# Mixture-of-experts units in another order: the units of two experts behind the three fixed ones, the five largest experts last

## The chip, the cores and the metric

One core of a Trainium2 chip runs the kernel. The metric is the device time of one execution in microseconds (us); lower is better. The kernel before takes 544.43 us, the median of three runs (543.29 to 544.66).

## The reference

One layer of a hybrid decoder trunk for 512 tokens of width 1024: a token-mixing part (convolution, RG-LRU and gated linear attention side by side), and then a mixture of 16 experts in 4 groups. Each token picks one group and two experts in it. Only the second part is touched by the change:

```python
def hier_moe(h, w_rg, b_rg, w_re, b_re, w_gate, w_up, w_down):
    ...
    y = jnp.zeros_like(h)
    for g in range(N_GROUPS):
        a = jnp.einsum("bsd,edf->bsef", h, w_gate[g])
        up = jnp.einsum("bsd,edf->bsef", h, w_up[g])
        hid = jax.nn.silu(a) * up * comb[:, :, g, :, None]
        y = y + jnp.einsum("bsef,efd->bsd", hid, w_down[g])
    return y
```

An expert has gate and up weights of 1024 x 512 and down weights of 512 x 1024, all in float32. The trunk's output is x plus both parts, with a last RMS norm.

## The kernel before

The first half of the time is the token mixing and the routing; the expert part runs from about 264 us to the end. On the chip the kernel counts how many tokens each expert has, sorts the thirteen experts that are not fixed by that count, and treats the experts as twelve **units**, one after the other (the loop over `u`, from about L1500):

- units 0 to 2 are the experts 0 to 2 (`NS` = 3, fixed, so that their weights can be loaded before the routing is known);
- units 3 to 7 are the five largest of the others (`NB` = 5), one expert each;
- units 8 to 11 are the eight smallest in pairs, 64 token slots for each of the two.

`alone(u)` tells a unit of one expert from a pair; `cols_of(u)` gives the ranks of a unit's experts, and the weights are named by rank: `raw_g40` is the first half of the gate weights of rank 4 (ranks 0 to 2 are the fixed experts), `raw_u` and `raw_d` are up and down.

**Weights.** An expert's weights are six chunks of 1 MB (two each of gate, up and down). All 96 chunks are loaded on SP's queue by `load_chunk` (L964) in the order in which the units use them, into a ring of 17 buffers (`nring`); a chunk's load is issued when the chunk 17 places before it has been used, and at most three loads (`AHEAD`) are in flight together.

**A unit of one expert** computes in split float32: every quarter of its weights is cast to a high part on ACT (`mh_...`, L87), and DVE takes the rest into a low part (`ml_...`, L88); the tokens are split likewise (`xh`, `xl`). Each product is three matmuls, high weights x high tokens (L82), low x high (L83) and high x low (L84). Of the down weights the last quarter stays plain float32 (L1449), save in the units that `full(u)` names. **A pair** uses the plain float32 weights as they were loaded: two experts' tokens stand side by side, 64 rows each, and each matmul works on one half of the columns of the PE array (`rows_of(a)`), gate and up at L1412, down at L1458. DVE splits nothing for a pair. In the trace a float32 matmul is two instructions.

**Order inside the loop.** In step `u`: gate projection of unit `u` into `pga`; the hidden values of unit `u-1` are turned (`pht`, L1420); up projection of unit `u` into `pup`; token slots and one-hots of unit `u+3` (`ptb`, `pwt`); the tokens of unit `u+1` are turned (`pgt`, L1381); the down projection of unit `u-1` (`pd`) and, from its result, `ye` on DVE (`scaled`, L1486) which is scattered to the tokens by GpSimd; then `sact` of unit `u`. The program is written in this order, but a scheduler sets the order of the instructions on each engine; an engine then works its own list strictly in that order.

**The end.** The last two units are not scattered: their results are put back into token order by matmuls with a one-hot matrix (`pf`, L1584), added to the rows read back from memory (`back_add`), normalised and stored. The down projection of the last unit is interleaved by hand with these.

Of the kernel before, what the change touches and what calls it, by code (L numbers as in the profile page):

```python
# [20 lines left out]
NT = T // P  # L21
# [3 lines left out]
KE = DE // P  # L25
# [12 lines left out]
NS = 3  # L38
NB = 5
ND = NE - NS  # L40
HALF = P // 2
HELD = 15
EARLY = 12


@with_exitstack
def trunk_kernel(
# [7 lines left out]
    nc = tc.nc  # L55
# [190 lines left out]
    for i in range(NT):  # L246
# [11 lines left out]
        for hf in range(2):  # L258
            pt = big(f"pxt{i}{hf}")
            for kk in range(4):  # L260
                k = hf * 4 + kk
# [110 lines left out]
    for kd in range(KD):  # L372
# [10 lines left out]
        if kd in (1, 2, 4):  # L383
            n = kd // 2 + 1
# [216 lines left out]
    both = range(2)  # L601
# [325 lines left out]

    NU = NS + NB + (ND - NB) // 2

    def alone(u):  # L930
        return u < NS + NB

    def cols_of(u):
        c = u if alone(u) else 2 * u - NS - NB
        return (c,) if alone(u) else (c, c + 1)

# [7 lines left out]
    raws = {}  # L946
# [183 lines left out]
    for i in range(NT):  # L1130
        for j in range(i + 1):
            nc.tensor.matmul(pp[:, i * NE:(i + 1) * NE], utri if j == i else onesb, chob[:, j, :],
                             start=(j == 0), stop=(j == i))
# [105 lines left out]
        nc.vector.tensor_reduce(swt[:, u:u + 1], pwt[:, 0:3], axis=AX.X, op=ALU.add)  # L1239

    def halves_of(u):
        n = 2 * (u - NS - NB)
        return shalf[:, n:n + 1], shalf[:, n + 1:n + 2]

    def unit_slots(u, oh):
# [43 lines left out]
    with tc.If(many > 0):  # L1289
        bcast(gt2, mod_dram[3])  # L1290
        with tc.tile_pool(name="ov", bufs=1) as ov:
# [6 lines left out]
            with tc.For_i(0, NE, 1) as e:  # L1298
# [12 lines left out]
                with tc.For_i(0, NT, 1):  # L1311
# [11 lines left out]
                    for hf in range(2):  # L1323
                        pt = small(f"ov_pt{hf}")
                        for kk in range(4):
                            k = hf * 4 + kk
# [34 lines left out]
    with ExitStack() as ms:  # L1361
        me = ms.enter_context(tc.tile_pool(name="me", bufs=2, reuse_waits="tile"))
        used = [0]
# [52 lines left out]
        def hid_t(u, hid):  # L1416
            pt = small(f"pht{u}")
            hv = hid.rearrange("s (p k) -> s p k", k=KE)
            for k in range(KE):
                nc.tensor.transpose(pt[:, k * P:(k + 1) * P], hv[:, :, k], ident)  # L1420
            pt = pt.rearrange("p (k t) -> p k t", k=KE)
            if not alone(u):
                ht = me.tile([P, KE, P], F32, tag="hh", bufs=2, name=f"ht{u}")
                nc.scalar.copy(ht, pt)  # L1424
                return None, None, ht
            n = KE if full(u) else KE - 1
            hh = me.tile([P, KE, P], F32R, tag="hh", bufs=2, name=f"hh{u}")[:, 0:n, :]
            hlo = me.tile([P, KE, P], F32R, tag="hlo", bufs=1, name=f"hlo{u}")[:, 0:n, :]
            nc.scalar.copy(hh, pt[:, 0:n, :])
            nc.vector.tensor_tensor(hlo, pt[:, 0:n, :], hh.bitcast(F32), ALU.subtract)  # L1430
            if full(u):
                return hh, hlo, None
            ht = me.tile([P, P], F32, tag="ht", bufs=1, name=f"ht{u}")
            nc.scalar.copy(ht, pt[:, KE - 1, :])
            return hh, hlo, ht

        def down(u, hs):

            ps = [big(f"pd{u}{i}") for i in range(2)]
            hh, hlo, ht = hs  # L1440

            def cols(hf):
                return slice(hf * 512, hf * 512 + 512)

            if alone(u):
                for k, (hi, lo) in enumerate(quarters()):
                    for hf in range(2):
                        if lo is None:
                            nc.tensor.matmul(ps[hf], ht, hi[:, 0, cols(hf)], start=False, stop=True)  # L1449
                        else:  # L1450
                            mm3(ps[hf], hh[:, k, :], hlo[:, k, :], hi[:, 0, cols(hf)], lo[:, 0, cols(hf)],
                                k == 0, k == KE - 1)
                    yield ps
                return

            def both(k, hf):
                for a in range(2):
                    nc.tensor.matmul(ps[hf][rows_of(a)], ht[:, k, rows_of(a)],  # L1458
                                     raws[used[0] + k // 2 * 2 + a][:, k % 2, cols(hf)],
                                     start=(k == 0), stop=(k == KE - 1))  # L1460
            if u == NU - 1:
                for hf in range(2):
                    for k in range(KE):
                        both(k, hf)
                        yield ps[hf]
                return
            for k in range(KE):
                for hf in range(2):
                    both(k, hf)
                yield ps  # L1470
            spent(4)
# [119 lines left out]
        def half15(hf, ps):  # L1591
            cols = slice(hf * 512, hf * 512 + 512)
            nc.vector.tensor_tensor(y15[:, cols], ps, gt2[:, cols], ALU.mult)
            part(p15, y15, hf)

        def back_add(i, hf):
            back(i, hf, oh15, p15, False)
            cols = slice(hf * 512, hf * 512 + 512)
            xi = xo[i][:, 0, cols]
            nc.vector.tensor_tensor(xi, xi, pf[i, hf], ALU.add)  # L1600
            nc.scalar.activation(xo[i][:, 1, cols], xi, AF.Square, scale=D ** -0.5, accum_out=sq[:, i, hf:hf + 1])
# [10 lines left out]
                nc.sync.dma_start(out[i * P:(i + 1) * P, cols], xo[i][:, 1, cols])  # L1612

        for n, ps in enumerate(down(NU - 1, hs)):
            if n % KE == KE - 1:
                half15(n // KE, ps)
            if n == KE + 1:
                for i in range(NT):
                    back(i, 0, oh14, p14, True)
            if n == KE + 2:  # L1620
                for i in (0, 1):
                    back_add(i, 0)
        for i in (2, 3):
            back_add(i, 0)
        for i in range(NT):
            back(i, 1, oh14, p14, True)
        for i in range(NT):
            back_add(i, 1)
# [37 lines left out]
```

## Time and profile before

| what | value |
|---|---|
| median of three runs | 544.43 us |
| the profiled execution, its own time | 542.79 us |
| its span, from the first instruction to the last | 541.1 us |
| mean granted TensorE clock | 0.976 |
| busy share of PE / DVE / ACT / POOL | 94% / 67% / 46% / 17% |
| moved by DMA | 164.58 MB, mean 304 GB/s |

The profiled execution lies 1.64 us under the median; its 542.79 us are 1.69 us more than its span, which is what lies around it. PE's share of 94% is an average over the whole kernel. The views shown further down are the page's forty slices (13.5 us each), the busy time of an engine in stretches, the timelines of PE and DVE (one row for each run of equal instructions, with the idle time ahead of it in brackets), what PE waited for, and the chain of work that ended last. Matmul ends in the timeline are modelled, so starts are the better numbers: in a run of equal instructions the step from one start to the next is the cost.

### The profile page before, as it was taken

What the parts mean: (1) busy time and instruction counts of PE and PEld (TensorE: products, weight loads), DVE (VectorE), ACT (ScalarE), POOL (GpSimd) and SP (SyncE); (2) the same over time, 40 slices, a digit from 0 to 9 for tenths busy, and PEclk for the clock granted to TensorE, in tenths of its full rate; (3) what the DMA queues carried; (4) which work ended last, traced back from release to release, by engine and by line L of the source; (5) the groups of instructions that cost most, each with busy time, mean ns of one, the idle gap of its engine ahead of it and who ended that gap; (6) DMA issues with size and microseconds to landing.
All of it is one profiled execution on the core that took longest, in us unless ns stands there. A gap on an engine that the chain in (4) does not pass through costs nothing.

```text
span 541.1 us, 7963 instructions
## 1 busy us (share of the span) xinstructions
PE 509.2 (94%) x2835; PEld 344.8 (64%) x2835; DVE 362.6 (67%) x654; ACT 248.4 (46%) x397; POOL 90.4 (17%) x126
## 2 busy tenths in 40 slices
PE   8999999999989999997889999999999999999891
PEld 7766766677657887766668777787876443342341
DVE  4544499999988747448799999999897121020227
ACT  5432587496126533334457768676774110000103
POOL 3311424000025100104110220120222010211002
PEclk9999999999999999996699999999999999999996
DMA  8995978748818399379899899999999999999963
GB/s 284 302 345 160 273 259 269 249 164 303 274 60 303 124 395 421 115 265 313 297 329 327 316 377 364 353 365 382 353 373 377 367 403 366 402 368 375 391 252 155
DMA packets 54304, 164.58 MB, mean 304 GB/s; under 512 B 12181, under 2 KB 30881, under 8 KB 39926
## 3 DMA queue, kind: packets, MB, share of 16 engines
q1 hardware_dynamic: 50710, 156.36, 78.9%
q0 software_dynamic: 3552, 7.69, 5.4%
q8 instruction: 23, 0.38, 0.3%
q14 instruction: 19, 0.16, 0.1%
HBM read 156.35 MB, written 12.62 MB: 312 GB/s over the span
## 4 chain that ended last, share of the span: by engine, by line
PE 28%; DMA 16%; DVE 5%; issue 1%; ACT 0%; POOL 0%; POOLq 0%; DVEq 0%; SPq 0%
DMA raw_u<-in_w_up_dram 7%; DMA raw_d<-in_w_down_dram 6%; DMA raw_g<-in_w_gate_dram 3%; PE pga L84 2%; PE pga L83 2%; PE pga L82 2%; PE pup L83 2%; PE pup L84 2%; PE pup L82 2%; PE pd L82 2%; PE pd L1449 2%; PE pd L83 2%; PE pd L84 2%; PE pd L1458 2%; PE pgt L1381 2%; PE pga L1412 1%
## 5 line engine op out<-in xcount | busy, mean ns | idle before, releaser
L507 DVE SCALAR_TENSOR_TENSOR cacc<-upad,vt,cacc 128x512 f32<-128x512 f32 x60 | 43.1, 755 | 0.1
L1536 DVE SCALAR_TENSOR_TENSOR sact<-pup,swt,sact 128x512 f32<-128x512 f32 x12 | 8.9, 745 | 50.1 <-PE pup L1412 50.1
L88 DVE TENSOR_TENSOR ml_u<-raw_u,mh_u 128x1024 fp32r<-128x1024 f32 x32 | 39.1, 1224 | 3.9 <-ACT mh_u L87 3.7
L87 ACT CAST mh_g<-raw_g 128x1024 fp32r<-128x1024 f32 x32 | 33.4, 1051 | 16.9 <-PE pga L84 12.3
L88 DVE TENSOR_TENSOR ml_g<-raw_g,mh_g 128x1024 fp32r<-128x1024 f32 x32 | 38.3, 1219 | 1.3 <-ACT mh_g L87 1.1
L87 ACT CAST mh_u<-raw_u 128x1024 fp32r<-128x1024 f32 x32 | 33.6, 1049 | 11.6 <-PE pga L84 9.4
L1458 PE MATMUL pd<-raw_d,ht 128*64 128x512 f32 x128 | 35.0, 600 | 1.5 <-DMA raw_d<-in_w_down_dram 1.5
L88 DVE TENSOR_TENSOR ml_d<-raw_d,mh_d 128x1024 fp32r<-128x1024 f32 x26 | 31.7, 1222 | 4.0 <-ACT mh_d L87 3.6
L1140 POOL DMA_INDIRECT gat<-h_rows,sidx x12 | 13.5, 1122 | 121.1 <-PE pgt L1381 68.9
L87 ACT CAST mh_d<-raw_d 128x1024 fp32r<-128x1024 f32 x26 | 27.3, 1049 | 8.1 <-PE pup L84 6.1
L1412 PE MATMUL pup<-raw_u,xh 128*64 128x512 f32 x128 | 29.4, 595 | 1.2 <-DMA raw_u<-in_w_up_dram 1.2
L1486 DVE TENSOR_TENSOR ye<-pd,gt 128x512 f32<-128x512 f32 x22 | 15.0, 690 | 21.8 <-PE pd L1458 20.3
L1412 PE MATMUL pga<-raw_g,xh 128*64 128x512 f32 x128 | 28.3, 594 | 0.0
L82 PE MATMUL pga<-mh_g,xh 128*128 128x512 f32 x64 | 27.4, 428 | 0.5 <-ACT xh L87 0.5
L83 PE MATMUL pup<-ml_u,xh 128*128 128x512 f32 x64 | 25.6, 400 | 1.6 <-DVE ml_u L88 1.5
L83 PE MATMUL pga<-ml_g,xh 128*128 128x512 f32 x64 | 26.1, 408 | 1.0 <-DVE ml_g L88 1.0
L84 PE MATMUL pga<-mh_g,xl 128*128 128x512 f32 x64 | 25.5, 399 | 0.4 <-DVE xl L88 0.4
L82 PE MATMUL pup<-mh_u,xh 128*128 128x512 f32 x64 | 25.8, 403 | 0.0
L84 PE MATMUL pup<-mh_u,xl 128*128 128x512 f32 x64 | 25.2, 394 | 0.0
L1458 PEld LDWEIGHTS pd<-raw_d,ht 128*64 128x64 f32 x128 | 10.8, 136 | 21.4 <-issue 16.8
L1084 POOL DMA_INDIRECT xo_rows<-ye,sidx x8 | 17.1, 2138 | 36.8 <-DVE ye L1486 36.8
L1424 ACT COPY ht<-pht 128x512 f32<-128x512 f32 x4 | 2.3, 586 | 43.0 <-PE pht L1420 43.0
(405 smaller groups left out, 1270.1 us busy)
## 6 DMA issues: line engine op xcount, KB each, us to landing
raw_g<-in_w_gate_dram SPq DMA_DIRECT2D x32, 1024.0 KB
raw_u<-in_w_up_dram SPq DMA_DIRECT2D x32, 1024.0 KB
raw_d<-in_w_down_dram SPq DMA_DIRECT2D x32, 1024.0 KB
wb<-in_w_ada_dram SPq DMA_DIRECT2D x16, 1024.0 KB
wa<-in_w_ada_dram SPq DMA_DIRECT2D x8, 512.0 KB
wa<-in_w_ada_dram SPq DMA_DIRECT2D x4, 1024.0 KB
raw_o<-in_w_out_dram SPq DMA_DIRECT2D x8, 512.0 KB
xin<-in_x_dram SPq DMA_DIRECT2D x4, 512.0 KB
```

The source lines that it names most:

```text
L82: nc.tensor.matmul(ps, lh, rh, start=start, stop=False)
L83: nc.tensor.matmul(ps, lh, rl, start=False, stop=False)
L84: nc.tensor.matmul(ps, ll, rh, start=False, stop=stop)
L87: one = nc.scalar.copy(hi, src)
L88: two = nc.vector.tensor_tensor(lo, src, hi.bitcast(F32), ALU.subtract)
L507: nc.vector.scalar_tensor_tensor(cacc[:, h, :], upad[:, h, t:t + T], w, cacc[:, h, :], ALU.mult, ALU.add)
L1084: nc.gpsimd.indirect_dma_start(out=xo_dram, out_offset=bass.IndirectOffsetOnAxis(ap=si, axis=0), in_=y, in_offset=None, bounds_check=T - 1 ...
L1140: return g, nc.gpsimd.indirect_dma_start(out=g, out_offset=None, in_=h2_dram, in_offset=bass.IndirectOffsetOnAxis(ap=sidx[:, e:e + 1], axi ...
L1381: nc.tensor.transpose(pt[:, kk * P:(kk + 1) * P], gv[:, :, k], ident)
L1412: nc.tensor.matmul(ps[rows_of(a)], xh[:, k, rows_of(a)], raws[used[0] + a][:, kk, :], start=(k == 0), stop=(k == KD - 1))
L1458: nc.tensor.matmul(ps[hf][rows_of(a)], ht[:, k, rows_of(a)], raws[used[0] + k // 2 * 2 + a][:, k % 2, cols(hf)], start=(k == 0), stop=(k = ...
L1486: nc.vector.tensor_tensor(y[:, cols], ps[hf], gt2[:, cols], ALU.mult)
```

## The change

The five largest experts move to the end of the list, and the four pairs come directly behind the fixed experts: units 0 to 2 fixed, 3 to 6 pairs, 7 to 11 one expert each, the largest in unit 7 (rank 3) and the smallest of the five in unit 11 (rank 7). The order of the weight loads follows, as it is made from the same list. `full(u)` is still `u % 4 == 3`, so that it now names units 3 (a pair, where it does nothing), 7 and 11. The last unit's down projection, which was that of a pair, is now of one expert and done in plain float32 with all 128 rows in the order of the new list `LAST`, without a split; the last unit's hidden values are therefore not split either. The `pf` matmuls of unit 10 are issued after four of the eight products of `LAST`. Line numbers behind the new code move by 2 to 11.

```diff
@@ -41,6 +41,8 @@
 HALF = P // 2
 HELD = 15
 EARLY = 12
+
+LAST = [(0, 0), (0, 1), (1, 0), (1, 1), (2, 0), (3, 0), (2, 1), (3, 1)]
 
 
 @with_exitstack
@@ -927,12 +929,15 @@
 
     NU = NS + NB + (ND - NB) // 2
 
+    NP = (ND - NB) // 2
+
     def alone(u):
-        return u < NS + NB
+        return u < NS or u >= NS + NP
 
     def cols_of(u):
-        c = u if alone(u) else 2 * u - NS - NB
-        return (c,) if alone(u) else (c, c + 1)
+        if alone(u):
+            return (u if u < NS else u - NP,)
+        return NS + NB + 2 * (u - NS), NS + NB + 2 * (u - NS) + 1
 
 
 
@@ -1239,7 +1244,7 @@
         nc.vector.tensor_reduce(swt[:, u:u + 1], pwt[:, 0:3], axis=AX.X, op=ALU.add)
 
     def halves_of(u):
-        n = 2 * (u - NS - NB)
+        n = 2 * (u - NS)
         return shalf[:, n:n + 1], shalf[:, n + 1:n + 2]
 
     def unit_slots(u, oh):
@@ -1419,7 +1424,7 @@
             for k in range(KE):
                 nc.tensor.transpose(pt[:, k * P:(k + 1) * P], hv[:, :, k], ident)
             pt = pt.rearrange("p (k t) -> p k t", k=KE)
-            if not alone(u):
+            if not alone(u) or u == NU - 1:
                 ht = me.tile([P, KE, P], F32, tag="hh", bufs=2, name=f"ht{u}")
                 nc.scalar.copy(ht, pt)
                 return None, None, ht
@@ -1442,6 +1447,12 @@
             def cols(hf):
                 return slice(hf * 512, hf * 512 + 512)
 
+            if u == NU - 1:
+                for k, hf in LAST:
+                    nc.tensor.matmul(ps[hf], ht[:, k, :], raws[used[0] + k // 2][:, k % 2, cols(hf)],
+                                     start=(k == 0), stop=(k == KE - 1))
+                    yield ps[hf]
+                return
             if alone(u):
                 for k, (hi, lo) in enumerate(quarters()):
                     for hf in range(2):
@@ -1458,12 +1469,6 @@
                     nc.tensor.matmul(ps[hf][rows_of(a)], ht[:, k, rows_of(a)],
                                      raws[used[0] + k // 2 * 2 + a][:, k % 2, cols(hf)],
                                      start=(k == 0), stop=(k == KE - 1))
-            if u == NU - 1:
-                for hf in range(2):
-                    for k in range(KE):
-                        both(k, hf)
-                        yield ps[hf]
-                return
             for k in range(KE):
                 for hf in range(2):
                     both(k, hf)
@@ -1612,17 +1617,16 @@
                 nc.sync.dma_start(out[i * P:(i + 1) * P, cols], xo[i][:, 1, cols])
 
         for n, ps in enumerate(down(NU - 1, hs)):
-            if n % KE == KE - 1:
-                half15(n // KE, ps)
-            if n == KE + 1:
+            if n == 3:
                 for i in range(NT):
                     back(i, 0, oh14, p14, True)
-            if n == KE + 2:
                 for i in (0, 1):
-                    back_add(i, 0)
+                    back(i, 1, oh14, p14, True)
+            if n in (5, 7):
+                half15(LAST[n][1], ps)
+        for i in range(NT):
+            back_add(i, 0)
         for i in (2, 3):
-            back_add(i, 0)
-        for i in range(NT):
             back(i, 1, oh14, p14, True)
         for i in range(NT):
             back_add(i, 1)
```

How the instructions stand now at the places that matter. First DVE where one unit's `ye` meets the next unit's first weight split. Before, at the end of step 3 (`ye2` is made from the down projection of unit 2, `pd20` and `pd21`; `ml_g400` and so on are the quarters of the gate weights of rank 4, that is of unit 4):

```order
L88 TENSOR_TENSOR ml_d210_3697<-raw_d21_3146,mh_d210_3696 128x1024
L88 TENSOR_TENSOR xl4_3657<-pgt40_3658,xh4_3656 128x512
L88 TENSOR_TENSOR xl4_3657<-pgt41_3665,xh4_3656 128x512
L88 TENSOR_TENSOR ml_g400_3724<-raw_g40_3168,mh_g400_3723 128x1024
L88 TENSOR_TENSOR ml_g401_3728<-raw_g40_3168,mh_g401_3727 128x1024
L1486 TENSOR_TENSOR ye2_3710<-pd20_3672,gt2_2604 128x512
L1486 TENSOR_TENSOR ye2_3710<-pd21_3673,gt2_2604 128x512
L88 TENSOR_TENSOR ml_g410_3746<-raw_g41_3214,mh_g410_3745 128x1024
```

Here the first two splits for the next unit stand ahead of `ye`. The same engine in the changed kernel at the end of step 6 (`ye5` from the down projection of the pair in unit 5; `ml_g300` is the first quarter of rank 3, unit 7):

```order
L134 TENSOR_SCALAR sidx_77<-ptb10_4269 128x1
L1244 TENSOR_REDUCE swt_78<-pwt10_4279 128x1
L1491 TENSOR_TENSOR ye5_4145<-pd50_4109,gt2_2604 128x512
L1491 TENSOR_TENSOR ye5_4145<-pd51_4110,gt2_2604 128x512
L90 TENSOR_TENSOR ml_g300_4162<-raw_g30_3926,mh_g300_4161 128x1024
L90 TENSOR_TENSOR ml_g301_4166<-raw_g30_3926,mh_g301_4165 128x1024
L90 TENSOR_TENSOR ml_g310_4184<-raw_g31_3985,mh_g310_4183 128x1024
```

Both halves of `ye` now stand ahead of every split of unit 7. Rows `ye6` and `ye7` stand in the same way ahead of the splits of units 8 and 9; at the last two steps one half of `ye` stands ahead of the first split and the other behind it.

Then PE in the down projection of a pair. Before, in step 9 (unit 8; `raw_d80` belongs to the first half of the columns, `raw_d90` to the second):

```order
L1381 MATMUL pgt101_4777<-ident_61,gat0_2602 128x128 x4
L1458 MATMUL pd80_4783<-raw_d80_4542,ht8_4733 64x512
L1458 MATMUL pd80_4783<-raw_d90_4552,ht8_4733 64x512
L1458 MATMUL pd81_4784<-raw_d80_4542,ht8_4733 64x512
L1458 MATMUL pd81_4784<-raw_d90_4552,ht8_4733 64x512
L1458 MATMUL pd80_4783<-raw_d80_4542,ht8_4733 64x512
```

The halves alternate, and the sixteen matmuls stand in one stretch of half-column work. In the changed kernel, in step 6 (unit 5; `raw_d12...` first half, `raw_d13...` second half):

```order
L1386 MATMUL pgt80_4287<-ident_61,gat0_2602 128x128 x3
L1469 MATMUL pd50_4109<-raw_d130_3912,ht5_4050 64x512
L1469 MATMUL pd51_4110<-raw_d130_3912,ht5_4050 64x512
L1469 MATMUL pd50_4109<-raw_d120_3892,ht5_4050 64x512
L1469 MATMUL pd50_4109<-raw_d130_3912,ht5_4050 64x512
L1469 MATMUL pd51_4110<-raw_d120_3892,ht5_4050 64x512
L1469 MATMUL pd51_4110<-raw_d130_3912,ht5_4050 64x512
L1386 MATMUL pgt80_4287<-ident_61,gat0_2602 128x128
L1386 MATMUL pgt81_4294<-ident_61,gat0_2602 128x128 x4
L1469 MATMUL pd50_4109<-raw_d121_3914,ht5_4050 64x512
L1469 MATMUL pd51_4110<-raw_d121_3914,ht5_4050 64x512
```

The down projection is now cut into stretches by transposes of full width, and a stretch can hold more matmuls of one half than of the other (here two of `raw_d120` and four of `raw_d130`; the two others of `raw_d120` stand further up, behind `pup`).

## Rows read from the trace of the kernel before

**Rows 1.** The page, part 2: busy tenths in 40 slices of 13.5 us.

```profile
PE   8999999999989999997889999999999999999891
PEclk9999999999999999996699999999999999999996
```

**Rows 2.** PE by stretch: us, PE busy (count), granted clock, DMA share, GB/s.

```profile
290.00:410.00 120.00, 119.93 (x618) 1.00 0.98 360
437.00:483.00 46.00, 46.00 (x220) 1.00 1.00 377
483.00:525.00 42.00, 39.19 (x149) 1.00 0.95 368
525.00:541.00 16.00, 4.82 (x20) 0.72 0.33 131
```

**Rows 3.** What PE waited for, 415 to 541 us: in total, times, longest.

```profile
PE pd L1458 <- DMA raw_d<-in_w_down_dram: 1.5, 2, 1.0
PE pup L1412 <- DMA raw_u<-in_w_up_dram: 1.2, 1, 1.2
```

**Rows 4.** Timeline of PE, step 11 and the end: start, us, line, operation, out<-in, count.

```profile
483.44 7.09 PE L1412 MATMUL pga<-raw_g,xh 128*64 128x512 f32 x32
...
515.89 1.43 PE L1584 MATMUL pf<-p,oht 128*128 128x512 f32 x5
517.25 1.07 PE L1458 MATMUL pd<-raw_d,ht 128*64 128x512 f32 x2
518.25 0.95 PE L1584 MATMUL pf<-p,oht 128*128 128x512 f32 x3
...
520.13 1.20 PE L1584 MATMUL pf<-p,oht 128*128 128x512 f32 x4
521.26 3.65 PE L1458 MATMUL pd<-raw_d,ht 128*64 128x512 f32 x12
```

**Rows 5.** Timeline of PE, step 9, and the down projection in step 10.

```profile
437.23 7.09 PE L1412 MATMUL pga<-raw_g,xh 128*64 128x512 f32 x32
444.24 0.75 PE L1420 MATMUL pht<-ident,sact 128*128 128x128 f32 x4
444.92 7.09 PE L1412 MATMUL pup<-raw_u,xh 128*64 128x512 f32 x32
451.94 1.16 PE L1381 MATMUL pgt<-ident,gat 128*128 128x128 f32 x8
453.02 7.09 PE L1458 MATMUL pd<-raw_d,ht 128*64 128x512 f32 x32
...
475.70 7.14 PE L1458 MATMUL pd<-raw_d,ht 128*64 128x512 f32 x32
```

**Rows 6.** Timeline of DVE between steps 4 and 5.

```profile
356.20 1.22 DVE L88 TENSOR_TENSOR ml_g<-raw_g,mh_g 128x1024 fp32r<-128x1024 f32 x1
357.43 1.29 DVE L1486 TENSOR_TENSOR ye<-pd,gt 128x512 f32<-128x512 f32 x2
358.63 2.35 DVE L88 TENSOR_TENSOR ml_g<-raw_g,mh_g 128x1024 fp32r<-128x1024 f32 x2
```

**Rows 7.** Timeline of PE at the same place.

```profile
357.69 0.40 PE L82 MATMUL pga<-mh_g,xh 128*128 128x512 f32 x1
357.93 0.39 PE L83 MATMUL pga<-ml_g,xh 128*128 128x512 f32 x1
```

**Rows 8.** DVE's busy time in step 5: us, busy (count), clock, DMA share, GB/s.

```profile
357.69:376.50 18.81, 17.98 (x23) 1.00 0.99 370
```

**Rows 9.** Timeline of PE, last quarter of a down projection in plain float32, 128 rows.

```profile
318.54 1.88 PE L1449 MATMUL pd<-raw_d,ht 128*128 128x512 f32 x4
```

**Rows 10.** The chain that ended last, 430 to 530 us: first and last of nine transfers.

```profile
434.02 8.52 DMA raw_g<-in_w_gate_dram
...
504.47 7.80 DMA raw_d<-in_w_down_dram
```

**Rows 11.** Timeline of SP's queue at the start of step 3.

```profile
319.84 1.27 SPq L964 DMA_DIRECT2D raw_d<-in_w_down_dram  x2
```

## The prediction

> **What bounds the kernel now.** The page's slices come first [rows 1]: PE is at nine tenths from the start of the expert part to the last slices, at the full granted clock up to the last one. PE by stretch [rows 2] says the same more sharply: 119.93 of 120 us busy in the stage of single experts, 46.00 of 46 in the first pair steps. So until 483 us time is matmul time, and only what makes PE's list longer or stops it can change the total. In the last pair step PE is idle for 2.8 of 42 us, and the list of waits names weight loads for all of it [rows 3]. In the last 16 us PE is busy for 4.82; that tail hangs on DVE, POOL and stores. DMA is at a share of 0.95 to 1.00 all along, so loads are the second bound: they catch up with PE in step 11. DVE is the third: 17.98 of 18.81 us busy in a step of one expert [rows 8], nearly free in a pair step.
>
> I take the sum as a difference against the profiled execution (542.79 us; span 541.1), which lies 1.64 under the median of 544.43, and add the result to the median. The same units run before and after, so the work cancels except for the parts below. A measurement of this kernel can tell about 0.3% from no change, that is 542.8 to 546.1.
>
> **1. What goes: the hungry last pair, -9.2.** From the first gate matmul at 483.44 to the end of the last weight matmul, 521.26 + 3.65 = 524.91, step 11 and the last down projection take 41.5 us [rows 4]. Undisturbed work: four stretches of 32 instructions at 7.01 us from start to start (437.23 to 444.24 [rows 5]) are 28.0; four transposes `pht` 0.7; the twelve `pf` matmuls in between 1.43 + 0.95 + 1.20 = 3.6. That is 32.3, so 9.2 are lost: 2.8 openly idle [rows 3], the rest inside the runs, where one half of the columns waited for its chunk, or stands alone (see 2). With single experts at the end six chunks are used in 18.8 us, 3.1 us each, while a chunk arrives every 2.90 us: nine links of three chunks in the chain from 434.02 to 512.27 [rows 10]. So no load is late there. Bounds: 7 (some of the interruptions by `pf` come back) to 10.
>
> **2. What the pairs cost in their new place, +7.7.** In a pair's stretch the halves run side by side: 32 instructions in 7.09 [rows 5]. What counts is the number of each half between two full-width instructions, not the order: the second half of the run at 475.70 has the halves doubled (first, first, second, second) and still takes 7.14 [rows 5]. But the last run, four instructions of one half and eight of the other, took 3.65, which is eight times 0.43 and the run's end, not six; and one matmul alone (2 instructions) holds PE from 517.25 to 518.25 [rows 4]. So a matmul without a partner costs 0.43 more than one with. In the changed order the transposes and the slot matmuls (`pht`, `pgt`, `ptb`, `pwt`) cut the pair work more often, as the PE rows of unit 5 show; added up over all stretches of units 3 to 6, twelve matmuls have no partner (before step 11: none): 12 x 0.43 = 5.2. There are about seven more excursions to full width. One costs what is left of the 0.68 us from `pht`'s start to `pup`'s when its transposes are taken off: eight `pgt` take 1.08, four `pht` 0.68, so four transposes are 0.40 and coming and going is 0.28, with the run's end 0.28 to 0.45; 7 x 0.35 = 2.5. Bounds 2.5 (only the excursions) to 9.
>
> By the Trainium skill, "TensorEngine Tiling (Array Packing)", Key Properties, tiles run independently and can load weights and multiply in parallel. By that sentence alone the lone matmuls would cost nothing extra and the sum below would be 5.2 lower, 547.5; the 3.65 us row says otherwise, and I follow the row.
>
> **3. New waits of PE for DVE, +8.5.** A matmul of a single expert needs the low part of its weights for the second of every three products. Before, the first split of the next unit runs while the old unit's down projection is still going, and `ye` follows it: 356.20 `ml_g`, 357.43 `ye` [rows 6], and PE goes from the high product at 357.69 to the low one at 357.93 without a gap [rows 7]. In the changed order both `ye` stand ahead of the first split. `ye` needs the end of the old down projection; then come 1.29 (two `ye`) and 1.22 (one split) [rows 6], against one high product of 0.24 that PE can do meanwhile [rows 7]: 1.29 + 1.22 - 0.24 = 2.3, of which about 0.1 is hidden as the first `ye` can start on the first half. So 2.2 at the step from 6 to 7 and 2.2 from 7 to 8. From 8 to 9 the order gives PE `pht` and four `pgt` ahead of the low product, some 1.1 us: 1.15 left. From 9 to 10 and 10 to 11 only one `ye` stands ahead (0.65 less): 0.55 each with `pht` as cover. Smaller ones of the same kind: the third quarter of the down weights now behind the token splits, three times 0.35; the last up to down hand-over of step 11 behind `sact` and the one-hots, 0.4; slots of unit 11 in step 7, 0.4 (estimates: about a third of a split's 1.22 each, as the rest lies under PE's lead). Together 8.5. Behind the waiting `ye` stand only DVE's own splits, and PE waits for these; in the pair stage DVE is idle, which helps nothing, as it keeps its list's order. DVE has only 0.8 us to spare in a step [rows 8], so it doesn't win back the lead soon. Bounds: 3 (only half of the two large ones and the third) to 10.5 (`sact` on ACT also late).
>
> **4. The last down projection in plain float32, +1.3.** Sixteen instructions at 0.43 (four in 1.88 with the run's end [rows 9]) are 6.9; the split one would be 24 matmuls at 0.235 [rows 7], 5.6.
>
> **5. At nothing.** Units 0 to 2 keep their order. The casts on ACT and DVE move with their units; one split of a down quarter falls away on DVE, which is not late there. Gathers and scatters on POOL's queue keep their number and fall under 18 to 23 us of step. The tail of 16.2 us from 524.9 to the span's end keeps its chain: last `ye`, split, `pf`, add, norm, store. Bound: 1 to either side. If its cover, the splits of the last `ye`, is late, it is the add that comes later.
>
> Sum: -9.2 + 7.7 + 8.5 + 1.3 = +8.3. The last weight matmul ends at about 533.2, the span at 549.4, the profiled execution would be 551.1, and against the median **552.7 us**. With the bounds taken together (not all at one end) 547 to 558.
>
> **Rivals.**
> *A, faster: alternating the stages pays.* The pairs, which need chunks fast and no DVE, stand between stages that need DVE and few chunks. If the scheduler's order costs PE nothing at the seams, because the low parts are ready in time, and only the excursions remain of 2: -9.2 + 2.5 + 1.3 = -5.4, 539.0. It decides at whether `ye` ends before PE reaches the first low product. The Trainium skill, "Perfetto Trace Analysis", Optimization Strategy, holds that kernels with several regimes may gain from interleaving them; by that rule this case holds. For it: the 2.8 us of open waiting go for certain. Against it: DVE's rows in the new order. Chance 0.14.
> *B, no change: the seams cost nothing, the lone matmuls do.* -9.2 + 7.7 + 1.3 = -0.2, 544.2. Chance 0.12.
> *C, more slower: loads fall behind in the pair stage.* At the start of step 3 the ring is full: the load issued at 319.84 [rows 11] is chunk 32, seventeen after the last one used (15), and lands some 4.4 us later. Four pair steps then use 46 chunks in about 96 us, 2.1 us each, against 2.90 [rows 10]. The last chunk of unit 5's down weights, 61, lands at 324.2 + 29 x 2.90 = 408.3 and is wanted at about 412 to 413. Beyond 3.05 us per chunk PE waits: at 3.15, 2.9 us, 555.6. Chance 0.11.
> *D, the clock.* In the tail, with PE busy for a third, the granted clock is 0.72; in the stretch with the waits of step 11 it stays 1.00 [rows 2]. Should it fall to the lower level at a seam and stay there for half a step, that costs about 9 us: over 560. Chance 0.06.
>
> **How the numbers follow.** The forecast has 0.57, A 0.14, B 0.12, C 0.11, D 0.06. The range 543 to 559 holds the forecast, B and C; A and D lie outside (0.20). The forecast's own range is 547 to 558. Faster is A, 0.14; within 0.3% is B, 0.12; slower is the rest, 0.74.
>
> **What would show it.** No PE wait for a weight load after 420 us (1); pair steps of 23.5 to 25 us in place of 22.7, with lone half-width matmuls 0.43 apart between transposes (2); gaps of about 2 us on PE right after the first high product of units 7 and 8, put down to DVE's `ml_g`, and DVE idle for PE's `pd` ahead of `ye` (3); the last eight weight matmuls 6.9 us (4); the last weight matmul near 533 and 16 us behind it (5). The prediction is wrong if the first low product of units 7 to 9 comes without a gap, or if step 7 begins near 411.

## The result, and the profile after

The changed kernel takes 550.0 us, the median of three runs (549.7 to 551.3), against 544.43 before: ratio 1.0118, 95% interval 1.0084 to 1.0151. It is slower by 5.6 us. The forecast was 552.7 in a range of 543 to 559. The span of the profiled execution is 548.3 us, 7.2 more than before.

The page's slices of the changed kernel, to set beside [rows 1] (13.7 us each): the thin slice in step 11 of the kernel before (the third from the end, from 500 us) has gone, and two others have come, from 411 and from 439 us, where units 7 and 8 begin.

```profile
PE   7999999999989999996899999999998989999991
PEclk9999999999999999996799999999999999999996
```

PE by stretch in the changed kernel (columns as in [rows 2]): the three fixed units, the pair steps 3 to 6, steps 7 to 10, step 11 to the last weight matmul, the tail.

```profile
290.00:320.70 30.70, 30.70 (x163) 1.00 0.94 348
320.75:420.00 99.25, 98.25 (x499) 1.00 1.00 385
420.00:502.50 82.50, 78.10 (x342) 1.00 1.01 381
502.50:532.00 29.50, 28.86 (x109) 1.00 0.55 199
532.00:548.00 16.00, 5.16 (x21) 0.75 0.33 131
```

PE is still busy nearly all the time, the granted clock is 1.00 up to the tail, and the tail is as long as before (16.0 us from 532.3 on, 16.2 before). What changed is where PE idles: before it waited for the weights of the last pair [rows 3]; now it waits for no load, and DVE stands in its place. The list of what PE waited for from 320 us on:

```profile
PE pga L85 <- DVE ml_g L90: 4.3, 4, 1.5
PE pht L1425 <- DVE xl L90: 0.7, 1, 0.7
PE pwt L1243 <- DVE sidx L134: 0.5, 2, 0.3
PE pd L1452 <- ACT ht L1429: 0.2, 1, 0.2
```

The timeline of PE in steps 6 and 7 shows both mechanisms that the prediction named:

```profile
399.86 1.07 PE L1417 MATMUL pup<-raw_u,xh 128*64 128x512 f32 x2
400.86 0.71 PE L1386 MATMUL pgt<-ident,gat 128*128 128x128 f32 x4
...
410.19 0.72 PE L1425 MATMUL pht<-ident,sact 128*128 128x128 f32 x4 [0.74 <-DVE xl L90]
...
412.11 3.65 PE L1469 MATMUL pd<-raw_d,ht 128*64 128x512 f32 x12
415.69 0.82 PE L1386 MATMUL pgt<-ident,gat 128*128 128x128 f32 x5
416.44 3.66 PE L1469 MATMUL pd<-raw_d,ht 128*64 128x512 f32 x16
...
420.03 0.49 PE L84 MATMUL pga<-mh_g,xh 128*128 128x512 f32 x1
422.05 0.50 PE L85 MATMUL pga<-ml_g,xh 128*128 128x512 f32 x1 [1.52 <-DVE ml_g L90]
```

Twelve instructions that a transpose cut off (four of one half, eight of the other) take 3.65 us, sixteen balanced ones right behind take 3.66: a matmul without a partner is paid in full. One alone holds PE for 1.0 us (399.86). At the seam into unit 7 the low product starts 2.02 us after the high one, where [rows 7] has 0.24. DVE's timeline there gives the reason; against [rows 6] `ye` and `ml_g` have changed places:

```profile
419.28 0.69 DVE L1491 TENSOR_TENSOR ye<-pd,gt 128x512 f32<-128x512 f32 x1 [7.51 <-PE pd L1469]
420.17 0.69 DVE L1491 TENSOR_TENSOR ye<-pd,gt 128x512 f32<-128x512 f32 x1 [0.19 <-PE pd L1469]
420.78 2.35 DVE L90 TENSOR_TENSOR ml_g<-raw_g,mh_g 128x1024 fp32r<-128x1024 f32 x2
```

DVE had been idle for 7.5 us, and for the last 2.4 of them the first split's inputs were at hand: ACT, which had waited for the load, made the first high part of unit 7 from 415.81 to 416.8 (two casts in 1.99):

```profile
415.81 1.99 ACT L89 CAST mh_g<-raw_g 128x1024 fp32r<-128x1024 f32 x2 [4.28 <-DMA raw_g<-in_w_gate_dram]
```

The end is what the prediction had: sixteen plain instructions with twelve `pf` in between, the last weight matmul at 532.3 (528.66 + 3.59).

```profile
519.69 1.13 PE L1452 MATMUL pd<-raw_d,ht 128*128 128x512 f32 x2 [0.20 <-ACT ht L1429]
...
523.30 2.74 PE L1452 MATMUL pd<-raw_d,ht 128*128 128x512 f32 x6
525.47 3.34 PE L1589 MATMUL pf<-p,oht 128*128 128x512 f32 x12
528.66 3.59 PE L1452 MATMUL pd<-raw_d,ht 128*128 128x512 f32 x8
```

### The profile page after: what moved, and what is told of

It reads as the page before. It is cut to its first block, busy times and chain, and to the rows that moved or that the text cites. A ratio compares the mean times of both kernels' runs of the same rounds, so it can differ in the third digit from the quotient of the medians.

```text
span 548.3 us, 7942 instructions
## 1 busy us (share of the span) xinstructions
PE 511.7 (93%) x2827; PEld 341.6 (62%) x2827; DVE 357.2 (65%) x653; ACT 244.2 (45%) x393; POOL 93.1 (17%) x128
## 4 chain that ended last, share of the span: by engine, by line
PE 41%; DVE 7%; issue 2%; ACT 1%; POOL 0%; POOLq 0%; DVEq 0%
PE pd L1469 6%; PE pup L1417 5%; PE pga L1417 5%; PE pga L85 2%; PE pup L85 2%; PE pga L86 2%; PE pup L86 2%; PE pup L84 2%; PE pgt L1386 2%; DVE ml_g L90 2%; PE pga L84 2%; PE pd L85 2%; PE pd L1460 2%; PE pd L86 1%; PE pd L84 1%
## 5 line engine op out<-in xcount | busy, mean ns | idle before, releaser
L1417 PE MATMUL pga<-raw_g,xh 128*64 128x512 f32 x128 | 30.2, 594 | 0.0
L90 DVE TENSOR_TENSOR ml_d<-raw_d,mh_d 128x1024 fp32r<-128x1024 f32 x22 | 26.8, 1222 | 2.4 <-ACT mh_d L89 2.3
L89 ACT CAST mh_d<-raw_d 128x1024 fp32r<-128x1024 f32 x22 | 23.0, 1052 | 6.7 <-PE pup L86 5.7
L86 PE MATMUL pga<-mh_g,xl 128*128 128x512 f32 x64 | 25.6, 400 | 0.1
L1089 POOL DMA_INDIRECT xo_rows<-ye,shalf x8 | 14.1, 1757 | 56.9 <-DMA xo_rows<-ye,shalf 36.4
L1089 POOL DMA_INDIRECT xo_rows<-ye,sidx x6 | 12.4, 2064 | 55.8 <-DVE ye L1491 46.8
```

The lines of the kernel that those rows point to most:

```text
L86: nc.tensor.matmul(ps, ll, rh, start=False, stop=stop)
L89: one = nc.scalar.copy(hi, src)
L90: two = nc.vector.tensor_tensor(lo, src, hi.bitcast(F32), ALU.subtract)
L1089: nc.gpsimd.indirect_dma_start(out=xo_dram, out_offset=bass.IndirectOffsetOnAxis(ap=si, axis=0), in_=y, in_offset=None, bounds_check=T - 1 ...
L1417: nc.tensor.matmul(ps[rows_of(a)], xh[:, k, rows_of(a)], raws[used[0] + a][:, kk, :], start=(k == 0), stop=(k == KD - 1))
```

## The experiments

The theory: the change takes away the hungry last pair (9 us) and pays more than that for cut pair stretches and for `ye` ahead of the splits. Its rivals: these two are one cost, or cost little, or the loads decide everywhere. Each kernel was timed beside the kernel before on the same chip; the ratio is to that kernel. These runs were made on several chips, where the kernel before had medians of 544.24 to 545.21, so a difference between the times of two experiments is good to about 1 us.

**ye behind the splits.** Only the order on DVE is put back, from unit 5 on.

```diff
-            y = scaled(u, ps)
+            if u + 1 >= NS + NP - 1:
+                with tc.issue_after(warmed.ins):
+                    for s in range(2):
+                        splits[used[0], s] = split_quarter(used[0], s)
+                with tc.issue_after(low_part[0].ins):
+                    y = scaled(u, ps)
```

> The changed kernel, with one difference: from unit 5 on, ye is put behind the first two splits of the next unit's gate weights on DVE, the order that the kernel before has. Theory (part 3 of the prediction, as sized by the trace of the change): the waits of PE for the first split at the starts of steps 7 to 11 are due to DVE's order alone. There PE loses 1.8, 1.7, 1.0 and some tenths; they go, and nothing takes their place: 550.0 - 5 = 545, between 544 and 546.5. First rival: the splits come no earlier, because the high part or the buffers of the low part are late too, so the same gaps stay: 549.5 to 550.5. Second rival: ye, now 2.5 us later, holds its PSUM bank longer and makes PE wait there: 547 to 550 with new waits of PE for ye.

Measured 545.45, ratio 1.0017 (1.0 to 1.0035). The waits for `ml_g` are gone from the list; what is left of it:

```profile
PE pht L1426 <- DVE xl L90: 0.7, 1, 0.7
PE pwt L1243 <- DVE sidx L134: 0.5, 2, 0.2
PE pd L1453 <- ACT ht L1430: 0.2, 1, 0.2
```

As expected: DVE's order at the seams costs 4.55 us by the two times, 5.5 by the two ratios and 4.9 by the two traces (from the start of step 7 to the last weight matmul 112.2 and 107.3 us). PE's list is the same up to the end of step 8, so that at the two large seams DVE's order is the cause; behind step 8 some transposes stand elsewhere too.

**ye ahead of the splits in the kernel before.** The same swap the other way, at the five seams into units 3 to 7.

```diff
-                with tc.issue_after(warmed.ins):
+                with tc.issue_after(warmed.ins), tc.issue_after(hold.pop().ins) if hold else ExitStack():
...
+            if NS <= u < NS + NB:
+                hold.append(made[0])
```

> The kernel before, with one difference: at the five seams into units 3 to 7 ye is put ahead of the first split of the next unit's gate weights on DVE, as the change's order has it (before, the splits stand first). It measures the seam's price by itself, in the old order of the units. Theory: 1.75 us at each seam, as at steps 7 and 8 of the changed kernel; in this stage the ring of weight buffers is full and the loads wait for PE, so later steps give nothing back: 544.4 + 8.7 = 553, between 551 and 554.5. Rival: the last pair waits for loads anyway, and a PE that gets there later waits less, so that the delay is taken up at the end: 544.5 to 548, with shorter waits for weights in step 11.

Measured 550.72, ratio 1.0107 (1.0072 to 1.0141). The order costs in the old place too: steps 3 to 7 take 101.9 us together in place of 95.5, the whole kernel 6.5 more. Nothing was given back at the end (step 11 and the last down projection take 42.2 in place of 41.5). A seam's price is 1.3, under the 1.75 expected:

```profile
PE pga L83 <- DVE ml_g L88: 5.6, 5, 1.3
```

**Pairs uncut.** Slot matmuls and transposes may come only between the projections of steps 3 to 7.

```diff
+        def behind(u):
+            return tc.issue_after(tail[0].ins) if NS <= u <= NS + NP else ExitStack()
...
-                hs = hid_t(u - 1, prev)
+                with behind(u if u <= NS + NP else u - 1):
+                    hs = hid_t(u - 1, prev)
...
+            with behind(u):
+                if u + 3 < NU:
+                    unit_slots(u + 3, hot)
...
+                with behind(u):
+                    xs = xtrans(u + 1, gat[(u + 1) % 2])
```

> The changed kernel, with one difference: in steps 3 to 7 (and for the pht of step 8) the slot matmuls and transposes may only come between the projections, as in the kernel before, so that no stretch of a pair is cut and every half-width matmul has its partner; the DVE order at the seams stays. Theory (part 2): cuts cost 12 lone matmuls x 0.43 and the excursions, 7.7; by the trace of the change steps 5, 6 and 7 hold 0.9 and about 9 us more than their work, so 550.0 - 9 = 541, between 539 and 543. PE's waits for the first split of units 7 and 8 remain. First rival: lone matmuls cost nothing extra (the halves are independent), only the excursions go: 547 to 548.5. Second rival: pair steps that are shorter by 9 us run into the weight loads: 544 to 548, with waits for weights in steps 5 to 7.

Measured 547.5, ratio 1.0065 (1.0044 to 1.0087): only 2.5 us won where 9 were expected. The time lies in the range of both rivals. Against the first, that lone matmuls cost nothing, stand the rows of 3.65 and 3.66 above. The cuts are gone, step 6 falls from 29.7 to 25.6 us, but the edit brought a wait of its own, and a load came late. Waits of PE, and two rows of its timeline:

```profile
PE pga L85 <- DVE ml_g L90: 3.6, 4, 1.3
PE pgt L1390 <- DVE sidx L134: 3.4, 5, 1.0
```

```profile
407.30 1.16 PE L1390 MATMUL pgt<-ident,gat 128*128 128x128 f32 x8 [0.62 <-DVE sidx L134]
408.38 8.69 PE L1473 MATMUL pd<-raw_d,ht 128*64 128x512 f32 x32
```

The transposes stand right behind the slot matmuls and wait there for DVE (3.4 us in five steps). And the down projection of unit 5, balanced and uncut, takes 8.69 and not 7.09 [rows 5]: its main part started 3.7 us earlier than in the changed kernel (412.11 above). The list of waits doesn't say why it is longer; with fewer loads it takes 7.09 (the shared weights below), so PE had reached the loads.

**Both edits together.** The two diffs above in one kernel.

> Both edits together: ye behind the first two splits, and no pair stretch cut. Theory (parts 2 and 3 add up): 550.0 - 9 - 5 = 536, between 534 and 538, faster than the kernel before by 1.2 to 1.9%. First rival (the loads become the bound once PE is 14 us faster): 540 to 544 and waits for weights. Second rival (the two gains are one, as the seams of steps 7 and 8 are where the cuts lie): 540 to 542.

Measured 544.69, ratio 0.9999 (0.9975 to 1.0023): as fast as before and not faster. The first rival comes nearest, with waits for weights, though 0.7 above its range. At the seam into unit 7 DVE now has the split first and still waits, for ACT, and ACT for the load:

```profile
416.53 2.36 DVE L90 TENSOR_TENSOR ml_g<-raw_g,mh_g 128x1024 fp32r<-128x1024 f32 x2 [7.05 <-ACT mh_g L89]
```

```profile
415.45 1.99 ACT L89 CAST mh_g<-raw_g 128x1024 fp32r<-128x1024 f32 x2 [6.81 <-DMA raw_g<-in_w_gate_dram]
```

**Slots behind the down projection.** The kernel with both edits, without the new wait that the uncut pairs brought.

```diff
-            with behind(u):
-                if u + 3 < NU:
-                    unit_slots(u + 3, hot)
...
+                if u + 3 < NU and NS <= u <= NS + NP:
+                    with behind(u):
+                        unit_slots(u + 3, hot)
```

> The kernel of uncut_and_behind, with one difference: in steps 3 to 7 the slot matmuls of unit u+3 come behind the down projection and no longer ahead of the transposes pgt, which waited there for a small PSUM bank until DVE had read the slots (3.4 us idle in five waits, some 4.5 with the drains). Theory: those waits go, but PE gets to the late weights of unit 5 and unit 7 that much earlier and waits for them: of 4.5 only those in steps 3 and 7 are kept, some 1.5 to 2: 542.5 to 543.5. Rival (loads are not the bound): the full 4.5, 540.

Measured 545.37, ratio 1.0019 (0.9997 to 1.0041). Nothing was won: against the kernel with both edits steps 3 to 5 are 2.3 us shorter together, and steps 6 to 8 are 2.9 longer. The slot waits are gone and loads stand in the list in their place:

```profile
PE pga L85 <- DVE ml_g L90: 2.9, 4, 1.1
PE pd L1474 <- DMA raw_d<-in_w_down_dram: 0.5, 1, 0.5
PE pup L1422 <- DMA raw_u<-in_w_up_dram: 0.4, 1, 0.4
```

**Shared weights, three times.** Without a quarter of the loads, in the kernel with both edits, the changed one and the one before.

```diff
+        if not alone(un) and c == cols_of(un)[1]:
+            raws[i] = raws[i - 1]
+            return
```

> The kernel of uncut_and_behind, with one difference: the second expert of every pair multiplies with the first one's weights, whose buffers it shares, so that 24 of the 96 weight loads fall away (the outputs of those experts are another sum); PE, DVE and ACT do the same work in the same order. Theory: in uncut_and_behind the loads have become the bound at the end of the pair stage (half of the down weights of unit 5 and the first gate weights of unit 7 came late). Without these loads step 6 falls from 25.5 to about 23.8, and the waits at the start of step 7 for ACT's and DVE's splits, which stood behind the load, go (about 1.5 in all): 544.7 - 3.5 = 541, between 540 and 542.5. Rival: the loads are not it, and PE's own waits for slots and transposes make up the whole rest: 544 to 545.5.

Measured 537.45, ratio 0.9871 (0.983 to 0.9911): 7.2 us under the same kernel with its loads, twice what was expected. From one first gate matmul to the next, step 6 falls from 25.5 to 23.8 us and step 7 from 23.3 to 21.1, which is 3.9 of it and about what was expected. The down projection of unit 5, 8.48 in the kernel with both edits, is back at its length:

```profile
407.73 7.09 PE L1477 MATMUL pd<-raw_d,ht 128*64 128x512 f32 x32
```

So it was a load that made it longer. Not all of the 7.2 is shown to be loads: the expectation that the order stays the same did not hold. PE's list is the same only up to the end of step 7, and DVE has three of the gate splits of unit 7 already in steps 5 and 6.

> The changed kernel, with one difference: the second expert of every pair uses the first one's weights, so that 24 of 96 loads fall away (the outputs of those experts are another sum). It asks whether loads cost the changed kernel anything. Theory: PE waits for no load there, and the cuts and DVE's order alone make it slow: 549 to 550.5. Rival (the loads already hold up the splits at the seams of steps 6 to 8, as they did when the pairs were uncut, where their removal gave 7.2): 544 to 547.

Measured 538.64, ratio 0.9893 (0.9859 to 0.9927), 11.4 under the changed kernel. This doesn't tell the theories apart: with fewer loads the scheduler itself made another list. In it DVE has the first two splits of unit 7 ahead of `ye5`, and the down projection of unit 5 is cut once and not twice. It suggests where the cuts came from: the scheduler reckons with late loads at that place and fills in what it has ready.

> The kernel before, with the same difference: the second expert of every pair uses the first one's weights, 24 loads fall away. It measures how much of the 9.2 us of part 1 were loads. Theory: the 2.8 openly idle and 1.5 to 2 hidden in stretches where one half waited: 544.4 - 4.5 = 540, between 538.5 and 541.5; lone matmuls and interruptions in the last down projection stay. Rival (nearly all of the 9.2 were loads, as the lone matmuls are themselves left over by waiting halves): 535 to 537.

Measured 532.75, ratio 0.9791 (0.9758 to 0.9825): 11.7 under the kernel before, the rival's side and beyond. The last weight matmul ends 9.6 us earlier, and step 11 with the last down projection takes 32.8 us, beside the 32.3 that part 1 called undisturbed. The last down projections are almost uncut. In the timeline forty instructions in one stretch take 0.22 each:

```profile
501.31 8.80 PE L1461 MATMUL pd<-raw_d,ht 128*64 128x512 f32 x40
```

The lone matmuls at the end have gone with the loads. But the scheduler's list of the last down projections is another one here too (the `pf` stand in groups of 8 and 4, not 5, 3 and 4), so how much a load held up and how much was the list isn't shown by this run.

**The last down projection split.** The change without its part 4.

```diff
-            if not alone(u) or u == NU - 1:
+            if not alone(u):
...
-            if u == NU - 1:
-                for k, hf in LAST:
...
+            if n == KE - 1:
+                for hf in range(2):
+                    half15(hf, ps[hf])
```

> The changed kernel, with one difference: the last unit's down projection is split like that of any other single expert in place of the plain float32 one, and both halves of the last ye come at its end. Theory (part 4): the down projection is 1.3 us shorter, but the tail loses the head start that the first half had, one ye and one split on DVE, about 1.4: no change, 549 to 551. Rival: DVE, which now has the four splits as well, makes PE wait in step 11 and the tail starts later: 551.5 to 554. Other rival: the tail hides the second half as before: 548 to 549.

Measured 549.97, ratio 1.0099 (1.0069 to 1.0129): no change, as expected.

**The new tail in the old order.** The last part of the change alone.

```diff
-                for hf in range(2):
-                    for k in range(KE):
-                        both(k, hf)
-                        yield ps[hf]
+                for k, hf in LAST:
+                    both(k, hf)
+                    yield ps[hf]
...
-            if n == KE + 1:
+            if n == 3:
```

> The change's last part alone: the order of the units as in the kernel before (the four pairs last), but the last pair's down projection goes through the new list LAST, and the pf matmuls of unit 10 stand together behind its fourth product, so that its second half is one uncut stretch, four matmuls of each half of the columns. Theory (part 1: of the 9.2 us that the last pair loses, part is lone matmuls and interruptions and no load): from the last late chunk at 512.3 there are 3.65 for the rest of the first half, 3.2 for twelve pf and 3.6 for eight paired matmuls: the last weight matmul ends near 522.8 in place of 524.9, and the tail stays: 544.4 - 2.1 = 542.3, between 541.5 and 543.5. Rival (the end hangs on the last chunk, or the tail grows since the first half's ye comes later): 544 to 545.5.

Measured 542.11 (12 runs), ratio 0.9957 (0.9935 to 0.9979): faster than both kernels, and as worked out. In its timeline the last late load releases PE at 514.50, in that execution 2.2 us later than before, and the rest takes 10.3 us where before it took 12.6. The first row is the kernel before, the others are the new tail:

```profile
512.31 3.65 PE L1458 MATMUL pd<-raw_d,ht 128*64 128x512 f32 x12 [0.51 <-DMA raw_d<-in_w_down_dram]
```

```profile
514.50 3.65 PE L1463 MATMUL pd<-raw_d,ht 128*64 128x512 f32 x12 [0.51 <-DMA raw_d<-in_w_down_dram]
518.08 3.06 PE L1588 MATMUL pf<-p,oht 128*128 128x512 f32 x12
521.07 3.70 PE L1463 MATMUL pd<-raw_d,ht 128*64 128x512 f32 x16
```

The last sixteen instructions stand in one balanced stretch of 3.70, and not in pieces of 2, 2 and 12 that take 1.07, 1.07 and 3.65 [rows 4].

**One single expert last.** Another list: four single ones, the pairs, the fifth single one.

```diff
-        return u < NS or u >= NS + NP
+        return u < NS + NB - 1 or u == NU - 1
```

> The changed kernel with another list: units 0 to 2 fixed, 3 to 6 the four largest experts, 7 to 10 the pairs, 11 the fifth largest, and at the one seam from a pair to a single expert ye stands behind the first two splits. Theory: what is right about the change (a last unit that needs few chunks in its time) stays, one seam is left of five, and the stage of pairs again meets a full ring, so the late loads come, if at all, in steps 9 and 10, with all but one single expert's work behind it: the last weight matmul is no longer than 4 to 5 us behind the last chunk, near 512 to 514: 518 to 521, 16.2 of tail, 537 to 540 as device time. Rival: the pair stage in steps 7 to 10 waits for loads as the last pair of the kernel before did, and the single unit's 19 us come on top: 541 to 545.

Measured 543.67, ratio 0.999 (0.9969 to 1.001): no gain; the time lies in the rival's range. The pair steps 8 to 10 are cut again; steps 8 and 9 take 23.3 and 23.5 us, step 10, which waits for a load as well (0.6 idle), 27.5, and the single unit's work comes on top.

**Halves apart.** The kernel before, four matmuls of one half first and then four of the other.

```diff
-                for kk in range(4):
-                    k = s * 4 + kk
-                    for a in range(2):
+                for a in range(2):
+                    for kk in range(4):
+                        k = s * 4 + kk
```

> The kernel before, with one difference: in the gate and up projections of a pair the four matmuls of one half of the columns come first and then the four of the other, in place of one by one. It measures how far the halves run independently in an uncut stretch. Theory (part 2: only the number of each half between two full-width instructions counts): no change, 543 to 546, and 32 instructions still take about 7.1. Rival (the engine takes instructions in order and a half waits its turn): a stretch of 8 matmuls, 4 and 4, takes up to 6.9 in place of 3.4, some 3 us more per projection, eight projections: 555 to 570.

One run, 552.64 beside 545.17. A projection takes 8.97 in place of 7.09, and the down projections, which were left alone, still 7.09:

```profile
418.27 8.97 PE L1412 MATMUL pga<-raw_g,xh 128*64 128x512 f32 x32
...
463.43 7.09 PE L1458 MATMUL pd<-raw_d,ht 128*64 128x512 f32 x32
```

Neither theory holds as it stood. (Eight projections at 1.9 would be 15 us; PE, which is later, waits for no load at the end, and step 11 with the last down projection takes 37.2 us in place of 41.5.) By the starts of the single instructions the extra 1.9 us are four that run alone at the start of the stretch and four at its end; between them the halves run side by side. So two matmuls of one half in a row cost nothing ([rows 5], 475.70), of four in a row some are paid. Only as long as the halves alternate that closely does nothing but their number in a stretch count.

## Why the prediction was right, and where not

The sign, the size (5.6 against 8.3) and the mechanisms came out; the last weight matmul ended at 532.3 where 533.2 was forecast. The parts:

1. **What goes, -9.2**: before_shared_weights moves the end by 9.6. The size was right. Its make-up stays open: the prediction gave part of it to lone matmuls and interruptions, which vanished in that run, but with another list. That some of it is the list and no load is shown by the new tail alone, which gets 2.3 back in the old order with all loads.
2. **Pairs in their new place, +7.7**: too small. Taking the other parts from the 7.3 by which the last weight matmul moved (9.2 back, less 4.55 to 5.5 for the seams, 1.3 for part 4, and 0.7 by which step 2 had become longer, 19.65 against 18.93, which no part foresaw) leaves 9 to 10, at or above the upper bound of 9. It is a remainder and not a measurement, as the uncut kernel brought waits of its own. Of the pair steps, forecast at 23.5 to 25 us, step 6 lies far outside: steps 3 to 6 take 22.2, 23.3, 24.1 and 29.7. Three small waits of the list above (0.7 and twice 0.25), which part 2 had not, are in the remainder; they come from `pht` and the slots, moved forward into a place where their inputs were just being made. With them the 7.7 become 8.9; up to 1 us stays open. That the order of the halves doesn't count was too wide a rule: it holds for two of one half in a row and not for four (8.97 for 32 instructions). Of the rule in the Trainium skill ("TensorEngine Tiling (Array Packing)", Key Properties) that tiles run independently, these runs bear out half: the halves do run side by side, but what one of them has left over when a full-width matmul follows is paid in full (412.11 against 416.44 above).
3. **DVE's order, +8.5**: too large by 3 to 4. Measured 4.55 to 5.5. Mis-sized was "about 0.1 is hidden as the first `ye` can start on the first half": the first half of `ye` was done at 419.97, before the down projection ended, so that 0.6 was hidden, and each of the two large seams cost 1.75 and not 2.2; the last two seams, forecast at 0.55 each, cost nothing and 0.35; of the smaller waits (1.85 together) only fractions show.
4. **Plain last down projection, +1.3**: the sixteen instructions take 6.9 as forecast; putting the split back ends the weight matmuls 1.1 us earlier (531.2) and changes nothing clear of noise in all (549.97), as the tail behind them is 0.6 longer.
5. **Tail and units 0 to 2**: the tail as forecast, step 2 longer by 0.7, for which no run here gives the cause.

The errors of 2 and 3 went opposite ways, so it is in part luck that the sum came closer than its parts. Rival C (loads fall behind) doesn't show in the result: PE waited for no load, and ACT had unit 7's first weights at 415.81, four us ahead of PE. But these four us, of which the first cast takes 1.0 and the first split 1.2, were all the margin there was, much as the prediction's 408.3 against 412 to 413 for the down weights of unit 5 said. This is why repairing both mechanisms gives 544.7 and not 536: the edits uncover the loads. Rival A, and with it the rule of the Trainium skill ("Perfetto Trace Analysis", Optimization Strategy) that interleaving regimes may help, holds in no run with all the loads: moving the pairs forward changed which of the two limits is felt, and the best version (542.11) keeps the old order. D did not occur: at the seams the granted clock stayed 1.00.

That the price of part 2 is caused by the cuts themselves is shown by the rows and by the shorter step 6 of the uncut kernel; how much the changed kernel would gain with no cut, no new wait and all its loads couldn't be tried apart from the loads and stays open.

## What to carry to other kernels

When both PE and the loads are near their limits, moving the hungry stage forward doesn't remove its hunger, it moves the place where it is felt, and a repair of everything else runs into it. Read the new order of each engine at every seam where a stage that needs a second engine begins: an instruction that waits for the end of the old unit must not stand ahead of one that the new unit needs first. And count half-width matmuls between two full-width ones: those without a partner cost double.

## What was not expected of the hardware

The two halves of the PE array go their own way only over a short distance: two matmuls of one half in a row cost nothing (7.14 for 32 in [rows 5]), four in a row 1.9 us a stretch of 32 (8.97). And the load pace hardly depends on who waits: in the kernel before, which idles on loads at the end, DMA is at a share of 0.95 there [rows 2], and in the changed one at 1.00 through the pair steps, with the first weights of unit 7 at the same time (415.8 and 415.5) in the changed kernel and in the one with both repairs, although PE was 3.5 us further in the second.
